# Small products of a hybrid RWKV-7, sparse and dilated attention trunk, laid out anew on the tensor array

## The chip, the cores and the metric

The kernel runs on one core of one Trainium2 chip. The core has a tensor engine (PE, with its weight loads shown as PEld), a vector engine (DVE), a scalar engine (ACT), a general engine (POOL) and a queue engine that issues most DMA transfers (SP). The metric is the device time of one execution in microseconds; a kernel's time is the median of its runs.

## What is computed

Two layers (DEPTH = 2) over 1024 tokens of width 1024, all in float32. Each layer projects the normalised input and feeds the columns to three branches, whose outputs are joined, projected and gated:

```python
for i in range(DEPTH):
    h = rms_norm(x, norm_g[i])
    z = h @ w_in[i]
    z_a, z_b, z_c = split_cols(z, (RWKV_IN_WIDTH, DSA_IN_WIDTH, DIL_IN_WIDTH))
    y_a = rwkv7_branch(z_a, ...)      # 6 heads of 64, a state of 64x64 per head, decay and rate by low-rank "lora"
    y_b = dsa_branch(z_b, ...)        # 4 heads of 64 on one key/value head; the 256 best keys of each query
    y_c = dilated_branch(z_c, ...)    # 3 groups of 2 heads, rates 1, 4, 16, blocks of 128
    x = x + jnp.concatenate([y_a, y_b, y_c], axis=-1) @ w_out[i]
    gate = jax.nn.sigmoid(rms_norm(x, ple_norm_g[i]) @ ple_w_gate[i])
    x = x + gate * (p[i] @ ple_w_proj[i])
return rms_norm(x, final_norm_g)
```

The products that matter here: in `dsa_branch` the scores `q k^T` (the query split in an upper and a lower part of its precision, so 64 features become 128 rows plus 64 more) and the probabilities times `v`; in `dilated_branch` the scores of a block of 128 queries with its own and the previous 128 keys; in `rwkv7_branch` the two lora products `tanh(wd) @ w_up` and `ad @ a_up`, and the scan over time, which is done in chunks of 64 tokens.

## The kernel before

**Stages of a layer.** (1) The tail of the previous layer and the first columns; (2) the projections of all other columns ("z", lines 713 to 737, each product as three of reduced precision), which fill PE until about 505 us in layer 1, beside the index scores and the search for each query's threshold on DVE and ACT (line 579, up to 433 us); (3) the mask of chosen keys on DVE (`dsa_mask`, lines 624 to 645); (4) the attention stage, from about 525 to 773 us: dilated attention (`dil_att`), attention over the chosen keys (`dsa_attend`), the rest of the RWKV chain, then `dil_join`; (5) the tail (line 1695), whose first product (line 334) needs `yT`, the joined outputs, back from memory.

**Who sets the order.** The work is written as streams of generators. `Flow.run` (line 182) plays them against assumed durations, the numbers in `piece(engine, us)`, and takes, among the streams that could start soon, the one of lowest `RANK` (line 38). What it yields is the fixed order of each engine's instructions; on the chip each engine works in this order and waits where an operand is late. `get` and `put` hand out buffers and PSUM banks by tag: "z" and "t" have 2 banks each, "a" has 4. `after` and `done` are events.

**The lines that the change touches.**
- DSA scores: lines 912 and 913, a product on 128 rows and one on 64 rows, for each head and up to 512 keys; 96 pairs in the two layers. Keys are loaded by `load_keys` (line 859).
- DSA values: line 970, probabilities (transposed, `pT`) stay in the array, 64 columns of `v` move; 288 products. Output: lines 976 to 998.
- Dilated scores: `turned` (line 1049) writes each head's queries with zeros in the other head's 64 rows, so that line 1065 uses all 128 rows; 48 units, 22 of them with a previous block (4 products), 26 without (2).
- Lora: line 1263 for the decay (rows 0 to 63), line 1275 for the rate (rows 64 to 127), both through `product` (record at line 1245), for each of 8 token blocks a layer.
- RWKV chain (`rwkv_chain`): for each token block two steps `e` of state read (line 1573), solve (1586) and state update (1596), and its outputs (1618). Lines 1378 (`rwkv_cross`), 1507 (`rwkv_merge`) and 1635 are not changed; they use parts of the array.
- Mask: lines 630 to 643, ten DVE instructions for each of six query blocks a layer.

Of the kernel before, what the change touches and what calls it, by code (L numbers as in the profile page):

```python
# [37 lines left out]
RANK = dict(chain=0, merge=28, inverse=2, cross=3, tokens=3, ahead=3, prep=-2, y=-1, out=6, counts=1.4, search=8,  # L38
            mask=18, products=36, evict=5.5, weights=2.5, embed=25, kept=35, columns=25, index=2, q=36, load=15,
# [64 lines left out]
def after(*event):  # L104
    return "after", event
# [98 lines left out]
def tile_kernel(ctx, tc, x, p, norm_g, w_in, tshift_mu, rwkv_w0, rwkv_w_up, rwkv_a0, rwkv_a_up, rwkv_k_k,  # L204
# [407 lines left out]
    def dsa_mask(mk, d):  # L612
# [11 lines left out]
        for qb in range(2, NT):  # L624
            n, j = (qb + 1) * 128, slice(qb - 2, qb - 1)
            hi, lo = d["hl"][qb]
            yield piece("DVE", 0.2 + n / 1900)
# [3 lines left out]
            DVE.tensor_scalar(tmp, lo, t[:, j], None, OP.is_equal)  # L631
            yield piece("DVE", 0.4 + 2.3 * n / 960)
            DVE.tensor_tensor(bias, bias, tmp, OP.mult)
            DVE.tensor_tensor_scan(tmp, zero.to_broadcast([128, n]), bias, need[:, j], OP.add, OP.subtract)
            yield piece("DVE", 1.45)
            DVE.tensor_scalar(tmp, tmp, 0.0, None, OP.is_ge)
            DVE.tensor_tensor(bias, bias, tmp, OP.mult)
            for src, lim in ((hi, T), (lo, t)):
                yield piece("DVE", 1.1)
                DVE.tensor_scalar(tmp, src, lim[:, j], None, OP.is_gt)  # L640
                DVE.tensor_tensor(bias, bias, tmp, OP.add)
# [9 lines left out]
    def z_streams(i, flow, wp, zp, HT, LT, col, feats, ZT, w1, wtail, d):  # L651
# [61 lines left out]
        def products(it):  # L713
# [5 lines left out]
            for x, c in enumerate(slices):  # L719
                for k in range(8):  # L720
                    if n:
                        yield after("w", 2, (n, k // 2))
                    if kind == "rwkv" or k % 2 == 0:
                        yield piece("PE", 0.7, True)
# [126 lines left out]


    def dsa_attend(flow, opened, d, gate):
# [5 lines left out]
        def load_keys(ka, dl, half):  # L859
# [4 lines left out]
            SP.dma_start(K[half][:64, 1].bitcast(F32), kd[:64, 1, c])  # L864
            SP.dma_start(V[half], vd[:, half * 4:half * 4 + 4])
# [35 lines left out]
        def scores(it):  # L901
# [6 lines left out]
            yield piece("PE", 0.05 + m / 600)  # L908
# [4 lines left out]
            PE.matmul(b, q[:64, h], k[:64, 1, :m], start=False, stop=True)  # L913
# [45 lines left out]
        def values(it):  # L959
            qb, h, c0 = it  # L960
            k0 = c0 // 128
            m = min(4, qb + 1 - k0)
            if h == 0 and k0 == 0:
                yield get("a")
            yield piece("PE", m * 0.214)
            if h == 0 and k0 == 0:
                O[qb] = psa()
            pT = PT.pop(it)
            for k in range(m):
                PE.matmul(O[qb][:, h * 64:(h + 1) * 64], pT[:, k * 128:(k + 1) * 128], V[k0 // 4][:, k],  # L970
                          start=k0 + k == 0, stop=k0 + k == qb)
# [4 lines left out]
        def output(qb):  # L976
            yield after("o", qb)
            yield piece("DVE", 1.03)
            st, sg, o = Q[qb]["st"], Q[qb]["sg"], O.pop(qb)
            DVE.reciprocal(st[:, 3], st[:, 2])  # L980
            y = da.tile([128, 256], F32, name="y")
            DVE.scalar_tensor_tensor(y.rearrange("p (h e) -> p h e", h=4), o[:, :256].rearrange("p (h e) -> p h e", h=4),
                                     0.5, st[:, 3].rearrange("p (h o) -> p h o", o=1).to_broadcast([128, 4, 64]),
                                     OP.mult, OP.mult)
            DVE.tensor_tensor(y, y, sg, OP.mult)
            yield piece("PE", 0.22)
            t = o[:, 256:]
            for j in range(2):
                PE.transpose(t[:, j * 128:(j + 1) * 128], y[:, j * 128:(j + 1) * 128], ident)
            yield piece("ACT", t_act(256))  # L990
            yt = d["dl"].tile([128, 256], F32, name="yt")
            ACT.copy(yt, t)
# [12 lines left out]

    hrow = lambda h: slice(h % 2 * 64, h % 2 * 64 + 64)


    def dil_att(flow, opened):
# [15 lines left out]
        def load(u):  # L1025
            nonlocal dl
            if u == 0:
# [3 lines left out]
                yield piece("POOL", 1.5)  # L1031
                for j in range(3):
                    QK.append(dl.tile([128, 3, 128], F32, name=f"qk{j}"))
                    POOL.memset(QK[j], 0.0)
# [14 lines left out]
        def turned(u):  # L1049
            yield get("qk")  # L1050
            yield piece("ACT", 0.77)
            qk, t = QK[u % 3], T.pop(u)
# [856 lines left out]
```

## Time and profile before

| | us |
|---|---|
| median of 3 runs | 1967.21 (1966.08 to 1974.93) |
| the profiled execution | 1961.57 |
| its span, first to last instruction | 1959.8 |
| PE busy | 1845.0 (94%) |
| DVE busy | 1287.7 (66%) |
| ACT busy | 1062.2 (54%) |
| POOL busy | 633.9 (32%) |
| mean granted clock of the tensor engine | 0.971 |

All profile rows name lines of the kernel ("L970" is line 970). A row of the timeline holds the start of a group of equal instructions, their time from the first start to the last end, the engine, line, operation, output<-inputs, for PE the part of the array used (rows*columns) and the shape, and the count; in brackets the idle time before it and what ended it. Products are pipelined: the time from one row's start to the next row's start is what PE spends on it. A float32 product leaves two records in the timeline, one of reduced precision leaves one.

### The profile page before, as it was taken

To read this page: it belongs to the slowest core of one execution; us is meant where nothing else is said; L and a number is where in the kernel's file an instruction comes from. 1 tells how busy PE (TensorE), PEld (TensorE's weight loads), DVE (VectorE), ACT (ScalarE), POOL (GpSimd) and SP (SyncE) were. 2 spreads that over 40 slices of the span, in tenths; PEclk is the share of its full clock that TensorE was granted. 3 is DMA by queue.
4 is the path that set the end of the run, shared out by engine and by line. 5 is a ranking of instruction groups with operands and counts; after the bars stand their busy time and mean duration, and the time that the engine had idled before them with its cause. 6 is when DMAs were issued, how large, how long until landed. Compare 5 with 4: busy or idle time off the path is not lost. (4 is left out here: it accounts for less than half of the span.)

```text
span 1959.8 us, 40297 instructions
## 1 busy us (share of the span) xinstructions
PE 1845.0 (94%) x15214; PEld 1687.6 (86%) x15214; DVE 1287.7 (66%) x2956; ACT 1062.2 (54%) x2377; POOL 633.9 (32%) x842
## 2 busy tenths in 40 slices
PE   7999999999799997899999999999998999969998
PEld 6888888999798886799998888899997988869998
DVE  4489998898765753215344889997986667432344
ACT  5576666662376864214246766665624868632323
POOL 5422263362232202223224322633613322112322
PEclk9999998999899998899999999999997999979999
DMA  6222323133353324612322223331323523164123
GB/s 195 62 68 88 112 84 101 55 89 98 115 160 96 96 67 137 215 44 66 113 93 60 73 87 105 99 90 52 104 92 111 175 81 108 42 206 130 44 81 114
DMA packets 232410, 196.36 MB, mean 100 GB/s; under 512 B 19284, under 2 KB 204056, under 8 KB 232216
## 3 DMA queue, kind: packets, MB, share of 16 engines
q1 hardware_dynamic: 232216, 193.79, 32.7%
q8 instruction: 120, 1.97, 0.4%
q14 instruction: 74, 0.61, 0.1%
HBM read 128.36 MB, written 65.37 MB: 99 GB/s over the span
## 5 line engine op out<-in xcount | busy, mean ns | idle before, releaser
L334 PE MATMUL z<-wH,HT 128*128 128x256 f32 x1024 | 291.9, 287 | 25.4 <-ACT HT L244 25.4
L735 PE MATMUL z<-wH,HT 128*128 128x256 f32 x1024 | 304.0, 297 | 9.7 <-DVE zt L778 8.2
L336 PE MATMUL z<-wH,LT 128*128 128x256 f32 x1024 | 294.3, 289 | 4.9 <-DVE LT L245 4.9
L335 PE MATMUL z<-wL,HT 128*128 128x256 f32 x1024 | 292.8, 287 | 0.0
L736 PE MATMUL z<-wL,HT 128*128 128x256 f32 x1024 | 291.2, 284 | 0.0
L737 PE MATMUL z<-wH,LT 128*128 128x256 f32 x1024 | 290.9, 284 | 0.0
L701 POOL TENSOR_TENSOR wL<-wraw,wH 128x512 fp32r<-128x512 f32 (+1 forms) x128 | 165.6, 1305 | 266.9 <-ACT wH L689 212.1
L334 PEld LDWEIGHTS z<-wH,HT 128*128 128x128 f32 x1024 | 198.8, 195 | 26.7 <-ACT HT L244 26.5
L735 PEld LDWEIGHTS z<-wH,HT 128*128 128x128 f32 x1024 | 197.3, 193 | 16.3 <-DVE zt L778 9.1
L336 PEld LDWEIGHTS z<-wH,LT 128*128 128x128 f32 x1024 | 198.8, 195 | 7.4 <-DVE LT L245 7.0
L335 PEld LDWEIGHTS z<-wL,HT 128*128 128x128 f32 x1024 | 199.5, 195 | 0.1
L736 PEld LDWEIGHTS z<-wL,HT 128*128 128x128 f32 x1024 | 197.7, 193 | 0.3
L737 PEld LDWEIGHTS z<-wH,LT 128*128 128x128 f32 x1024 | 197.4, 193 | 0.0
L326 POOL TENSOR_TENSOR wL<-wraw,wH 128x512 fp32r<-128x512 f32 (+1 forms) x72 | 100.5, 1414 | 282.4 <-ACT wH L325 267.9
L735 PE MATMUL z<-HT,wH 128*128 128x512 f32 x416 | 165.6, 398 | 0.4 <-DVE zt L757 0.4
L736 PE MATMUL z<-LT,wH 128*128 128x512 f32 x416 | 162.9, 392 | 0.0
L737 PE MATMUL z<-HT,wL 128*128 128x512 f32 x416 | 162.7, 391 | 0.0
L325 ACT CAST wH<-wraw 128x512 fp32r<-128x512 f32 (+1 forms) x72 | 46.8, 650 | 137.6 <-PE z L336 91.8
L579 DVE TENSOR_SCALAR_CACHE_REDUCE junk<-hi,t 128x384 bf16<-128x384 uint16 (+3 forms) x136 | 110.3, 811 | 3.9
L1566 POOL TENSOR_TENSOR sp<-S,PC 64x192 f32<-64x192 f32 x64 | 33.2, 519 | 243.1 <-DVE S L1600 240.7
L579 DVE TENSOR_SCALAR_CACHE_REDUCE junk<-lo,t 128x384 bf16<-128x384 uint16 (+3 forms) x136 | 109.8, 807 | 3.0
L475 DVE SCALAR_TENSOR_TENSOR sc<-rl,iw,sc 128x512 f32<-128x512 f32 (+3 forms) x140 | 106.8, 809 | 2.5 <-ACT rl L462 0.4
(297 smaller groups left out, 4640.0 us busy)
## 6 DMA issues: line engine op xcount, KB each, us to landing
wraw<-in_w_in_dram SPq DMA_DIRECT2D x208, 128.0 KB
zr<-zt SPq DMA_DIRECT2D x52, 256.0 KB
zd<-zt SPq DMA_DIRECT2D x48, 256.0 KB
z<-zd SPq DMA_DIRECT2D x48, 256.0 KB
wraw<-in_w_out_dram SPq DMA_DIRECT2D x32, 256.0 KB
pd<-pe SPq DMA_DIRECT2D x32, 256.0 KB
hn<-yT SPq DMA_DIRECT2D x16, 512.0 KB
wraw<-in_ple_w_gate_dram SPq DMA_DIRECT2D x32, 256.0 KB
```

What stands on the lines that cost most here:

```text
L325: ACT.copy(H[:, :, :n], raw)
L326: POOL.tensor_tensor(L[:, :, :n], raw, H[:, :, :n].bitcast(F32), OP.subtract)
L334: PE.matmul(o, aH, bH, start=j == 0, stop=False)
L335: PE.matmul(o, aH, bL, start=False, stop=False)
L336: PE.matmul(o, aL, bH, start=False, stop=j == n - 1)
L475: DVE.scalar_tensor_tensor(sc[:, c], rl, w, sc[:, c], OP.mult, OP.add)
L579: DVE.tensor_scalar(junk[0][:, :n], hl[qb][lower], col(t, qb), None, OP.is_lt, OP.add, accum_out=col(cnt, qb))
L701: POOL.tensor_tensor(L, RAW.pop(it), H.bitcast(F32), OP.subtract)
L735: PE.matmul(o, aH, bH, start=k == 0, stop=False)
L736: PE.matmul(o, aH, bL, start=False, stop=False)
L737: PE.matmul(o, aL, bH, start=False, stop=k == 7)
L1566: POOL.tensor_tensor(sp[hrow(h)], s0[hrow(h), :, hrow(h)], PC[hrow(h), :, e:e + 1].to_broadcast([64, 3, 64]), OP.mult)
```

## The change

- DSA scores: the second product uses all 128 rows; the upper half of that part of the keys is set to zero once per 512 keys, on POOL.
- DSA values: `v` (64 columns) stays in the array and the transposed probabilities move; two heads go to the upper and lower 64 output rows of one bank. The sum is then already transposed; the gate and the reciprocal are multiplied before the transposes, and the result after them.
- Dilated scores: no zeros; the two heads use rows 0 to 63 and 64 to 127 and write two "a" banks.
- Lora: one block of six products that alternate between the row halves, into two "t" banks.
- State update: six products of 64 output rows instead of three of 128; outputs: one block of twelve products for both halves instead of two of six, at rank 18 instead of -1; the state's part of the output is copied to `Yt` (now 2 buffers) at once.
- Mask: four pairs of DVE instructions become one each; the loads of the attention stages get rank 1.8 instead of 15.
- The assumed durations of these pieces are changed with them.

```diff
-            mask=18, ... y=-1, ... load=15, ...
+            mask=18, ... y=18, ... load=1.8, ...
...
             DVE.tensor_scalar(bias, hi, T[:, j], None, OP.is_equal)
-            DVE.tensor_scalar(tmp, lo, t[:, j], None, OP.is_equal)
-            DVE.tensor_tensor(bias, bias, tmp, OP.mult)
+            DVE.scalar_tensor_tensor(bias, lo, t[:, j], bias, OP.is_equal, OP.mult)
...
-                DVE.tensor_scalar(tmp, src, lim[:, j], None, OP.is_gt)
-                DVE.tensor_tensor(bias, bias, tmp, OP.add)
+                DVE.scalar_tensor_tensor(bias, src, lim[:, j], bias, OP.is_gt, OP.add)
...
+            POOL.memset(K[half][64:, 1].bitcast(F32), 0.0)
...
             PE.matmul(b, q[:, h], k[:, 0, :m], start=True, stop=False)
-            PE.matmul(b, q[:64, h], k[:64, 1, :m], start=False, stop=True)
+            PE.matmul(b, q[:, h], k[:, 1, :m], start=False, stop=True)
...
-                PE.matmul(O[qb][:, h * 64:(h + 1) * 64], pT[:, k * 128:(k + 1) * 128], V[k0 // 4][:, k],
-                          start=k0 + k == 0, stop=k0 + k == qb)
+                for e in range(2):
+                    PE.matmul(O[qb][hrow(e), h // 2 * 128:h // 2 * 128 + 128], V[k0 // 4][:, k],
+                              pT[e][:, k * 128:(k + 1) * 128], start=k0 + k == 0, stop=k0 + k == qb)
...
-            for h in range(2):
-                ACT.copy(qk[hrow(h), h], t[hrow(h), :128])
-            ACT.copy(qk[:, 2], t[:, 128:])
+            ACT.copy(QK[u % 3], T.pop(u).rearrange("p (j t) -> p j t", j=2))
...
-            yield get("a")
+            yield get("a", 2)
...
-                    PE.matmul(B[u][:, h, e * 128:e * 128 + 128], QK[u % 3][:, h], QK[(u - 1 + e) % 3][:, 2],
+                    PE.matmul(B[u][h][:, e * 128:e * 128 + 128], QK[u % 3][hrow(h), 0], QK[(u - 1 + e) % 3][hrow(h), 1],
                               start=True, stop=True)
...
-            yield from product(lambda pr: lora[:64, fc(pr)], lambda pr: wa[:64], "ACT", 0.8, tanh(P, "w0"))
+            for pr in range(3):
+                for e in range(2):
+                    PE.matmul(b[e][:, fc(pr)], lora[hrow(e), fc(pr)], wa[hrow(e)], start=True, stop=True)
...
-                for pr in range(3):
-                    PE.matmul(b[:, fc(pr)], BKt[:, e, fc(pr)], SV[:, e, fc(pr)], start=True, stop=True)
+                for h in range(6):
+                    PE.matmul(up[hrow(h), h // 2], BKt[:, e, hcol(h)], SV[:, e, hcol(h)], start=True, stop=True)
...
-            for e in range(2):
-                yield after("sa", hf, e)
-                for h in range(6):
+            yield after("sa", hf, 1)
+            for h in range(6):
+                for e in range(2):
                     PE.matmul(b[kr(e), hcol(h)], G[:, e, h, kr(e)], SV[:, e, hcol(h)], start=True, stop=True)
```

Since the planner's numbers change, the whole order moves. In the changed kernel's rows the lines are shifted: L974 is the values' product, L1050, L1065, L1101 and L1120 are the dilated turn, scores, transposes and values, L1585, L1600, L1612 and L1629 are the chain's read, solve, update and outputs, L1689 and L1188 are the last transposes of RWKV and of the join.

PE at the end of layer 1's attention stage, before: the last DSA values (L970), the join's and RWKV's transposes, then the tail's first product.

```order
L1187 MATMUL t<-cst,o 128x128 x3
L970 MATMUL a<-v,pT 128x64 x4
L1187 MATMUL t<-cst,o 128x128 x3
L970 MATMUL a<-v,pT 128x64 x4
L1679 MATMUL t<-cst,o_9116 128x128 x3
L1187 MATMUL t<-cst,o 128x128 x3
L970 MATMUL a<-v,pT 128x64 x4
L1187 MATMUL t<-cst,o 128x128 x3
L970 MATMUL a<-v,pT 128x64 x4
L1187 MATMUL t<-cst,o 128x128 x6
L989 MATMUL a<-cst,y 128x128 x2
L334 MATMUL z<-wH,HT 128x256
```

The same place in the changed kernel:

```order
L1600 MATMUL a<-rs,TT 64x64 x6
L1101 MATMUL a<-cst,dpr 128x128 x2
L1612 MATMUL a<-SV,BKt 64x64 x6
L1629 MATMUL a<-SV,G 64x64 x12
L1120 MATMUL a<-z,dpT 128x64 x2
L1050 MATMUL t<-cst,z 128x128 x2
L1065 MATMUL a<-qk_5836 128x128 x2
L1101 MATMUL a<-cst,dpr 128x128 x2
L1120 MATMUL a<-z,dpT 128x64 x2
L1689 MATMUL t<-cst,o_9195 128x128 x3
L1188 MATMUL t<-cst,o 128x128 x24
L334 MATMUL z<-wH,HT 128x256
```

The DSA values no longer stand between the join's transposes; the last dilated unit and the last step of the RWKV chain do stand directly before them.

DVE at the end of the last mask block of layer 1, before: L641 and L640 are of the mask, L643 writes its result; the rest belongs to the RWKV chain (L1578, L1600, L1620), its preparation (L1382) and its output (L1673).

```order
L640 TENSOR_SCALAR junk_635<-lo_624,t 128x1024
L641 TENSOR_TENSOR junk_634<-junk_634,junk_635 128x1024
L1600 TENSOR_TENSOR S_1930<-a,sp 64x3x64 x2
L1382 TENSOR_TENSOR G<-t,cst 128x2x2x128
L1673 TENSOR_TENSOR o_5097<-Yt,ost 128x384
L1578 TENSOR_TENSOR rs<-a,gv 64x384
L1382 TENSOR_TENSOR G<-t,cst 128x2x2x128
L1620 TENSOR_TENSOR Yt<-a,rs 64x384
L643 TENSOR_SCALAR hi_623<-junk_634 128x1024
L1620 TENSOR_TENSOR Yt<-a,rs 64x384
L1600 TENSOR_TENSOR S_1929<-a,sp 64x3x64 x2
```

In the changed kernel L633 to L638 are the mask, L640 writes its result, L1548 and L1556 are of the merge, L775 of the projections, and L1592 and L1615 are the chain:

```order
L633 SCALAR_TENSOR_TENSOR junk_635<-zero,lim,junk_634 128x1024
L635 SCALAR_TENSOR_TENSOR junk_634<-junk_635,junk_634 128x1024
L638 SCALAR_TENSOR_TENSOR junk_634<-hi_623,T,junk_634 128x1024
L1548 TENSOR_TENSOR TT<-t,DT 128x384
L638 SCALAR_TENSOR_TENSOR junk_634<-lo_624,t,junk_634 128x1024
L775 SCALAR_TENSOR_TENSOR zt<-zt,z 128x512
L640 TENSOR_SCALAR hi_623<-junk_634 128x1024
L1556 TENSOR_TENSOR TT<-TT,t 128x384
L1592 TENSOR_TENSOR rs<-a,gv 64x384
L1615 TENSOR_TENSOR S_1951<-a,sp 64x3x64 x2
L775 SCALAR_TENSOR_TENSOR zt<-zt,z 128x512
L1592 TENSOR_TENSOR rs<-a,gv 64x384
```

The first chain step of the second pair of token blocks, with all that follows it, now stands behind the last mask block.

More of the change, by code (lines that the diff above doesn't have):

```diff
@@ L36 @@
 RW, DS, DL = 0, 1664, 2600
-RANK = dict(chain=0, merge=28, inverse=2, cross=3, tokens=3, ahead=3, prep=-2, y=-1, out=6, counts=1.4, search=8,
-            mask=18, products=36, evict=5.5, weights=2.5, embed=25, kept=35, columns=25, index=2, q=36, load=15,
+RANK = dict(chain=0, merge=28, inverse=2, cross=3, tokens=3, ahead=3, prep=-2, y=18, out=6, counts=1.4, search=8,
+            mask=18, products=36, evict=5.5, weights=2.5, embed=25, kept=35, columns=25, index=2, q=36, load=1.8,
             dil=20, join=8, dsa=65)
@@ L626, in dsa_mask @@
             hi, lo = d["hl"][qb]
[L627 removed]
+            yield piece("DVE", 0.2 + n / 770)
             bias, tmp = (a[:, :n] for a in d["junk"])
@@ L1080, in biased @@
             for h in range(2):
-                DVE.tensor_tensor_reduce(pr[:, h, lo:], b[:, h, lo:], mask, -0.125, ROOF, OP.add, OP.min,
+                DVE.tensor_tensor_reduce(pr[:, h, lo:], b[h][:, lo:256], mask, -0.125, ROOF, OP.add, OP.min,
                                          accum_out=o[:, 128 + h:129 + h])
+            yield put("a")
             yield put("a")
@@ L1259, in decay @@
             yield done("w", hf)
-            lora, wa, P, iP = R["lora"], T["wa"], tile_("P"), tile_("iP")
+            lora, wa, P, iP, ta, ke = R["lora"], T["wa"], tile_("P"), tile_("iP"), tile_("ta"), tile_("ke")
             yield piece("ACT", 0.24)
             ACT.activation(wa[:64], wa[:64], AF.Tanh)
-            yield from product(lambda pr: lora[:64, fc(pr)], lambda pr: wa[:64], "ACT", 0.8, tanh(P, "w0"))
+            yield get("t", 2)
+            yield piece("PE", 0.9)
+            b = pst(), pst()
+            for pr in range(3):
+                for e in range(2):
+                    PE.matmul(b[e][:, fc(pr)], lora[hrow(e), fc(pr)], wa[hrow(e)], start=True, stop=True)
+            yield piece("ACT", 0.8)
+            tanh(P, "w0")(b[0])
+            yield put("t")
+            yield piece("ACT", 0.8)
+            tanh(ta, "a0")(b[1])
+            yield put("t")
+            yield done("rate", hf)
             yield piece("DVE", 1.25)
@@ L1272, in icl @@
         def icl():
-            yield after("w", hf)
-            lora, wa, ta, ke = R["lora"], T["wa"], tile_("ta"), tile_("ke")
-            yield from product(lambda pr: lora[64:, fc(pr)], lambda pr: wa[64:], "ACT", 0.8, tanh(ta, "a0"))
+            yield after("rate", hf)
+            ta, ke = T["ta"], T["ke"]
             yield piece("DVE", 1.6)
@@ L1825, in tile_kernel @@
             rk = Pools(None)
-            flow = Flow(t=2, z=2, a=4, raw=3, wHL=2, zt=3, iqS=2, rl=4, sc=2, wk=1, w=1, rv=1, AR=2, BK=2, gv=1, t2=2, G=2, SV=2, BKt=1, XN=1, rs=3,
-                        Yt=1, dz=3, qk=3, dpr=1, dpT=2, pe=3, O=3, qload=2, pr=5, pT=4)
+            flow = Flow(t=2, z=2, a=4, raw=3, wHL=2, zt=3, iqS=2, rl=4, sc=2, wk=1, w=1, rv=1, AR=2, BK=2, gv=1, t2=2, G=2, SV=2, BKt=1, XN=1, rs=2,
+                        Yt=2, dz=3, qk=3, dpr=1, dpT=2, pe=3, O=3, qload=2, pr=5, pT=4)
             flow.free.update(BUSY)
```

92 lines of the change are left out of this document (46 added, 46 removed).

## The prediction

> **What bounds the kernel now.** I read the page first, then the busy time in windows, then the timeline of PE, because a product's rate stands only in the distance between starts: the "mean ns of one" of a pipelined product is its delay.
>
> ```profile
> span 1959.8 us, 40297 instructions
> PE 1845.0 (94%) x15214; PEld 1687.6 (86%) x15214; DVE 1287.7 (66%) x2956; ACT 1062.2 (54%) x2377; POOL 633.9 (32%) x842
> ```
>
> ```profile
> 150.00:200.00 50.00, 50.00 (x221) 41.20 (x220) 45.13 (x92) 33.59 (x58) 13.69 (x23) 1.00 0.28 84
> 200.00:250.00 50.00, 48.13 (x283) 42.03 (x282) 47.25 (x120) 33.97 (x67) 14.67 (x19) 1.00 0.37 107
> 600.00:650.00 50.00, 48.44 (x493) 42.30 (x489) 32.29 (x98) 34.38 (x105) 11.94 (x17) 1.00 0.33 91
> 750.00:800.00 50.00, 31.81 (x204) 30.30 (x202) 14.38 (x28) 16.33 (x29) 12.82 (x11) 0.73 0.63 195
> 850.00:900.00 50.00, 50.00 (x422) 50.00 (x421) 17.77 (x22) 18.06 (x33) 18.30 (x25) 1.00 0.15 49
> ```
>
> The columns are span, PE, PEld, DVE, ACT, POOL, granted clock. PE is full nearly everywhere. From 600 us to 650, the attention stage, it has 48.44 of 50 us and no other engine over 35: a microsecond of PE taken out there is one of the span, until something else is late. Around 200 us DVE (47.25) is as full, from the search. At the layer's end (750 to 800) PE waits and its clock falls to 0.73. Full windows give rates: 221 products of 512 columns in 50 us are 0.226 us each, 422 of 256 columns 0.118.
>
> **The change part by part: prices.**
>
> ```profile
> 586.12 0.92 PE L1507 MATMUL t<-DT,XN 64*64 64x64 f32 x24
> 586.86 0.87 PE L1507 MATMUL t<-XN,rs 64*64 64x64 f32 x24
> 635.65 0.91 PE L1618 MATMUL a<-SV,G 128*64 128x64 f32 x12
> 636.50 0.55 PE L1401 MATMUL t<-cst,zv 128*128 128x128 f32 x3
> 637.10 0.83 PE L1596 MATMUL a<-SV,BKt 128*128 128x128 f32 x6
> 637.86 0.91 PE L1618 MATMUL a<-SV,G 128*64 128x64 f32 x12
> 646.08 0.93 PE L1245 MATMUL t<-wa,lora 64*128 64x128 f32 x6
> 646.94 0.33 PE L1416 MATMUL t<-cst,BK 128*128 128x128 f32 x1
> ...
> 661.42 1.16 PE L1378 MATMUL t<-AR,BK 64*128 64x128 f32 x16
> 662.51 0.44 PE L1100 MATMUL a<-cst,dpr 128*128 128x128 f32 x2
> 663.06 0.51 PE L912 MATMUL z<-kq,q 128*128 128x512 f32 x1
> 663.50 0.50 PE L913 MATMUL z<-kq,q 64*128 64x512 f32 x1
> 663.93 0.66 PE L1119 MATMUL a<-z,dpT 128*128 128x64 f32 x4
> 664.42 1.06 PE L970 MATMUL a<-v,pT 128*128 128x64 f32 x8
> 665.31 0.39 PE L1047 MATMUL t<-cst,z 128*128 128x128 f32 x2
> 666.21 0.31 PE L912 MATMUL z<-kq,q 128*128 128x128 f32 x1
> 666.45 0.32 PE L913 MATMUL z<-kq,q 64*128 64x128 f32 x1
> 666.70 0.43 PE L970 MATMUL a<-v,pT 128*128 128x64 f32 x2
> ```
>
> "64*128" is the part of the array used, rows by columns. A float32 product leaves two records. Whole array: L970's eight take 0.89 us, 0.111 a record. Two products on different rows share the time: L1378's 16 records on alternating halves take 1.09, not 16 x 0.111 = 1.78. Of the 1.09, 16 x 0.056 = 0.90 is the products; 0.19 is extra. The four records of L1119 after L913 take 0.49, not 0.44, so a neighbour pays too. I price an isolated block of another array form at 0.3 us (0.19 plus 0.1 around it, an estimate). The Trainium skill, "TensorEngine Tiling (Array Packing)", Key Properties, says that changing the tiling mode drains the engine; by that it speaks for the scores and against the values, the state update and the dilated scores, and the trace agrees. Were the change of form free, the scores would gain nothing and the values, lora, outputs, state update and dilated scores, at the overlapped rate alone, 32 + 11 + 11 + 10 + 16 = 80 us.
>
> - **DSA scores on full rows.** A pair of 512 columns takes 0.44 + 0.43 us, two plain products 2 x 0.226 = 0.45: 0.42 saved, x48. At 128 columns 0.24 + 0.25 against 2 x 0.111: 0.27, x16. The 32 pairs of 256 and 384 columns lie between, 0.35. Sum 20.2 + 4.3 + 11.2 = 36 us. The two clears of half a key tile run on POOL, idle two thirds of the time, and precede a load: zero.
>
> ```profile
> L970 PE MATMUL a<-v,pT 128*128 128x64 f32 x576 | 82.3, 284 | 1.4 <-ACT pT L956 1.4
> ```
>
> - **Values transposed.** 288 products (576 records) of 0.223 are 64 us. Now 64 columns of V stay and 128 columns of pT move; two heads use the two column halves. No row shows such a pair. From below: both halves together take one whole-array product's time, 144 x 0.223 = 32. From above: no overlap, 64. I take the overlap, since L1507, whose tiles differ in rows and columns, runs 24 records in 0.74 us where L1618 on one half needs 0.85 for 12. With 48 blocks at 0.3 (14 us) the gain is 32 - 14 = 18 us; the other end is a loss of 14.
> - **Outputs.** Two blocks of 0.85 us become one of 24 records, which by L1507 takes 0.80 with its changes: 0.9 and a neighbour's 0.1 saved, x16 = 16 us. Without overlap 2.
> - **Lora.** Two blocks of 0.86 + 0.1 become one of 12 records, by L1378 1.09 - 4 x 0.056 = 0.87, + 0.1: 0.95 x 16 = 15 us. The second tanh now stands earlier on ACT, behind nothing that is late.
> - **State update.** 0.76 us for six records becomes 12 of half width: 0.19 + 6 x 0.062 (L1507's 0.74/12) + 0.1 = 0.66: 0.1 x 32 = 3 us. Without overlap 1.04, a loss of 9.
> - **Dilated scores.** Eight records 0.89 become 0.29 + 0.45 (22 blocks); four, 0.44, become 0.29 + 0.22 (26): +3 - 2 = 1 us. ACT saves two copies a unit; no wait there is long enough to count.
> - **Ranks, slots, Yt.** L1618's counterpart still stands right behind the chain's step in the order: zero. The loads' rank moves only SP issues: zero.
>
> The sum on PE is 36 + 18 + 16 + 15 + 3 + 1 = 89 us. Blocks that stand beside each other share a change: I take 90.
>
> **Mask on DVE.**
>
> ```profile
> 432.77 0.16 DVE L588 TENSOR_TENSOR lim<-cnt,lim 128x6 f32<-128x6 f32 x1
> 522.62 0.41 DVE L643 TENSOR_SCALAR hi<-junk 128x1024 bf16<-128x1024 bf16 x1
> ```
>
> ```profile
> L604 DVE SCALAR_TENSOR_TENSOR lo<-hi,T,lo 128x1024 uint16<-128x1024 uint16 x2 | 2.6, 1284 | 0.1
> L641 DVE TENSOR_TENSOR junk<-junk,junk 128x1024 bf16<-128x1024 bf16 x4 | 2.8, 692 | 0.1
> L1578 DVE TENSOR_TENSOR rs<-a,gv 64x384 f32<-64x384 f32 x32 | 17.8, 555 | 24.6 <-ACT rs L1576 24.2
> ```
>
> Four pairs of instructions become four joined ones. By L604 a joined one costs 1.28 us at 1024; a pair costs L641's 0.69 and a compare, bounded by L643's 0.41 and by another 0.69. So -0.1 to +0.2 each, 48 of them: -5 to +9 us on DVE, taken as zero. More matters where the mask stands: from the search's end (432.77) to the last mask (522.62) pass 90 us, and in the new order the chain's steps, a preparation and an output that stood between (four L1578 at 0.56, and some twenty more of like size) come behind it: 24 x 0.56 = 13 us of work, and the waits for PE before it. I put the mask's end 13 to 20 us earlier. The dilated stage, gated by it, starts earlier beside the last projections. That is what lets the saving of the first half of a layer, where DVE is full, count at all.
>
> **Given back at the layer's end.**
>
> ```profile
> 740.78 0.29 DVE L1127 TENSOR_TENSOR O<-a,z 128x128 f32<-128x128 f32 x1 [0.32 <-PE a L1119]
> ...
> 750.50 0.17 DVE L1156 TENSOR_TENSOR w<-o 128x16 f32<-128x16 f32 x1 [2.84 <-DMA o<-od]
> 752.32 0.18 DVE L1157 TENSOR_TENSOR w<-w,o 128x16 f32<-128x16 f32 x1 [1.65 <-DMA o<-od]
> ```
>
> ```profile
> 753.54 0.66 PE L947 MATMUL a<-cst,pr 128*128 128x128 f32 x4 [2.96 <-ACT pT L956]
> ...
> 782.06 0.58 PE L334 MATMUL z<-wH,HT 128*128 128x256 f32 x1 [9.22 <-ACT HT L244]
> ```
>
> Now the last dilated unit ends at 741, its sums travel to memory and back until 752.3, and DSA products fill PE meanwhile; PE loses 2.96 us at 753 and 9.22 before the tail. In the new order DSA's values end before the last two dilated units and the last chain step; after the last unit PE has only 27 transposes (3 us). Its 11.5 us of travel, about 4 of weights and first transposes, and the 9 before the tail then stand bare: 24 - 3 = 21 us idle, now some 15 with the slowed clock. The two last units, with nothing between their steps, add about 6. So 12 us a layer, 0 to 20, are lost: 2 x 12 = 24 us off the 90. I take 22, since the mask's earlier end helps the start of the stage.
>
> The forecast is 90 - 22 = 68 us. The profiled execution took 1961.57 us, its span 1959.8; the median of the runs is 1967.2, 5.6 higher, and I expect the same distance after. 1967.2 - 68 = 1899 us.
>
> **The rivals.**
>
> 1. *The end exposes nothing more* (the sums' travel falls on the chain's last steps): the whole 90 us, 1877. Against it stands the order itself. 12%.
> 2. *Column halves overlap in part or not at all.* Values lose up to 32 us, outputs 14, state 12: gain 68 - 58 = 10 at worst, about 20 since the longer PE work covers the end; half of it gives 39. So 1913 to 1947. For it: no row shows two tiles that differ in columns alone. Against: L1507. 12%. The Trainium skill, "TensorE: Matmul & The Clock Gate", Part 3, lists 2.38 times for three column tiles; an estimate of 1.6 for two would cut the gain by about 14 us, to 1913.
> 3. *The RWKV chain binds instead of PE.*
>
> ```profile
> PE a L1586 <- DVE rs L1578: 10.6, 15, 2.5
> ```
>
> ```profile
> 607.97 0.78 PE L1573 MATMUL a<-S,AR 128*128 128x128 f32 x5
> 718.93 0.78 PE L1573 MATMUL a<-S,AR 128*128 128x128 f32 x5
> ```
>
>    Between the two starts, of the third and fourth pair of token blocks, lie 111 us. In the new order about 85 us of PE work stands between them. If preparation, inverse and merge take 100 us whatever PE does, 15 us a layer are lost: a gain of 36, 1931. For it: that chain runs through DVE, ACT and POOL in small steps. Against: the longest of PE's waits for it is 2.5 us, so PE, not the chain, was late. 13%.
> 4. *Slower: banks.* The dilated scores now take two of the four "a" banks at once, which DSA's transposes and outputs and the chain use too. PE works in order, so a block without its second bank holds all that follows.
>
> ```profile
> PE a L947 <- ACT pT L956: 6.1, 2, 3.1
> ```
>
>    That is the longest wait on an "a" bank's readers now, 3 us. At 3 us in each of the 48 blocks the kernel would lose 146 against 68 gained: 2045. It decides from 1.4 us a block. Against: banks are given out by the same planner. 3%.
> 5. *No change*: rivals 2 and 3 together, gain under 10 us: 3%.
>
> **How the numbers follow.** The forecast's own case (gain 51 to 84 us, 1883 to 1916) has 57%. The range leaves out rival 4, no change, and the far ends of 1 and 2: 1875 to 1936. About 0.5%, 10 us, is what a measurement here tells from no change. Faster: 57 + 12 + 12 + 13 = 94%; same 3%; slower 3%.
>
> **What would show it.** Right: score pairs near 0.45 us; eight records of values near 0.45 to 0.5 us plus the change; 24 output records in 0.8; the tail's first product near 748 us instead of 782, after an idle of PE over 15 us; the last mask before 512 us. Wrong: values records at 0.11 each (rival 2); PE under 46 of 50 us in the attention windows with chain steps waited for (rival 3); waits before the dilated scores (rival 4).

## The result and the profile after

The changed kernel takes 1920.3 us in the median (1919.5 to 1924.5), the kernel before 1968.8 in the runs beside it: a ratio of 0.9754, 95% interval 0.9726 to 0.9782, or 48 us saved. The forecast was 68. Beside the later runs the kernel before came out at 1968.2 to 1969.3, so medians from different rounds are set against each other below. The profiled executions lie closer together (1961.6 and 1924.5, 37 us), because the one before was below its median and the one after was the highest of its runs.

The page of the changed kernel, the span and the busy times:

```profile
span 1922.7 us, 40427 instructions
PE 1764.9 (92%) x15406; PEld 1606.5 (84%) x15406; DVE 1278.8 (67%) x2892; ACT 1038.0 (54%) x2281; POOL 639.2 (33%) x840
```

PE is busy for 80 us less, but the span is only 37 shorter: 43 us of new idle time. To see where, I cut layer 1 at the first state read of each pair of token blocks (L1573 before, L1585 after) and at the tail's first product. Busy time in these stretches, before (columns: stretch, its length, PE, PEld, DVE, ACT, POOL, granted clock, DMA share, GB/s):

```profile
0.00:370.20 370.20, 346.70 (x2275) 306.88 (x2276) 287.07 (x609) 234.59 (x464) 152.00 (x227) 0.99 0.33 99
370.20:495.20 125.00, 121.89 (x1254) 116.43 (x1253) 109.31 (x248) 58.64 (x129) 46.26 (x60) 1.00 0.27 82
495.20:608.00 112.80, 101.64 (x1014) 91.59 (x1012) 75.70 (x205) 72.26 (x200) 36.63 (x42) 0.92 0.45 136
608.00:718.90 110.90, 109.12 (x1077) 92.90 (x1076) 74.53 (x251) 81.53 (x237) 21.91 (x29) 1.00 0.32 91
718.90:782.00 63.10, 48.78 (x397) 42.83 (x396) 26.28 (x71) 28.79 (x68) 14.58 (x18) 0.87 0.37 105
```

and after:

```profile
0.00:362.80 362.80, 334.18 (x2179) 295.73 (x2180) 277.57 (x595) 226.90 (x452) 141.46 (x215) 0.98 0.33 97
362.80:495.60 132.80, 126.61 (x1338) 121.17 (x1337) 124.08 (x248) 64.55 (x140) 60.18 (x72) 0.99 0.29 87
495.60:601.50 105.90, 100.92 (x1150) 90.23 (x1149) 69.67 (x203) 73.39 (x199) 36.07 (x40) 0.97 0.54 162
601.50:700.00 98.50, 89.01 (x1048) 72.43 (x1048) 72.32 (x234) 70.50 (x188) 22.26 (x29) 0.98 0.29 80
700.00:763.70 63.70, 37.97 (x398) 30.78 (x396) 24.08 (x72) 30.36 (x73) 17.80 (x20) 0.77 0.45 128
```

The second stretch became longer (125 to 133 us; DVE is busy for 124.08 of them), the third and fourth shorter by 7 and 12, and the last kept its length although PE has 11 us less to do there: it waits 26 of 64 us. The stretches are cut at events and hold different work before and after (see the counts), so a longer stretch alone doesn't say that PE lost time in it.

Three numbers for each kernel make this exact. From all records of PE: its busy time, each record counted until the next one starts; of that, half of what lies in stretches where the granted clock is 0.5 is called **half clock**, the rest **work**; what lies between records is **idle**. Their sum is 18 to 19 us under the span (the head and the end). The positions are of layer 1, in us: p1 to p4 are the state reads named above, then the first and the last values product of the dilated units, and the tail's first product.

| kernel | median | ratio to before (95%) | work | idle | half clock | p1 | p2 | p3 | p4 | dilated | tail |
|---|---|---|---|---|---|---|---|---|---|---|---|
| before | 1968.8 | 1 | 1805.0 | 96.0 | 40.0 | 370 | 495 | 608 | 719 | 544-740 | 782 |
| changed | 1920.3 | 0.9754 (0.9726-0.9782) | 1723.4 | 139.9 | 41.5 | 363 | 496 | 602 | 700 | 512-735 | 764 |
| *parts alone* | | | | | | | | | | | |
| e1_scores | 1948.9 | 0.9911 (0.9881-0.9941) | 1782.8 | 111.3 | 31.8 | 367 | 492 | 601 | 711 | 540-740 | 775 |
| e2_values | 1965.8 | 0.9988 (0.9970-1.0007) | 1784.5 | 114.9 | 44.2 | 367 | 492 | 607 | 726 | 543-742 | 784 |
| e3_rwkv | 1977.7 | 1.0044 (1.0015-1.0072) | 1770.3 | 127.4 | 51.7 | 369 | 510 | 626 | 737 | 535-741 | 787 |
| e4_dil | 2021.7 | 1.0260 (1.0189-1.0332) | 1806.8 | 119.7 | 64.6 | 368 | 493 | 605 | 712 | 547-788 | 811 |
| e5_mask | 1976.6 | 1.0056 (1.0035-1.0076) | 1807.5 | 96.5 | 51.6 | 367 | 497 | 615 | 734 | 528-740 | 789 |
| *one part left out* | | | | | | | | | | | |
| e10_no_dil | 1943.9 | 0.9873 (0.9799-0.9948) | 1729.0 | 147.9 | 38.5 | 363 | 496 | 613 | 724 | 519-718 | 768 |
| e7_no_rwkv | 1943.2 | 0.9888 (0.9841-0.9934) | 1764.0 | 129.7 | 28.7 | 367 | 497 | 615 | 715 | 513-744 | 780 |
| e8_no_mask | 1963.0 | 0.9971 (0.9948-0.9994) | 1722.4 | 158.8 | 65.7 | 369 | 510 | 623 | 731 | 531-764 | 789 |
| e11_no_lora | 1918.9 | 0.9746 (0.9711-0.9781) | 1739.5 | 119.5 | 43.0 | 366 | 487 | 599 | 705 | 516-741 | 766 |
| *order and clock* | | | | | | | | | | | |
| e6_oldranks | 1948.3 | 0.9897 (0.9832-0.9962) | 1728.4 | 148.0 | 53.6 | 362 | 499 | 610 | 715 | 512-752 | 780 |
| t1_dil_first | 1973.2 | 1.0022 (0.9988-1.0056) | 1724.2 | 169.8 | 59.1 | 362 | 495 | 628 | 743 | 510-737 | 789 |
| f1_warm | 1919.0 | 0.9750 (0.9721-0.9779) | 1753.3 | 109.1 | 37.5 | 362 | 495 | 601 | 699 | 511-734 | 766 |

The profiles are one execution each. f1_warm keeps the changed kernel's order and adds products at the layers' ends, and its stretch from the tail to layer 2's first state read came out with 7 us less idle and half clock than the changed kernel's. Part of that may be the added products' effect, so such sums can carry up to some 7 us. Its work holds 30 us of the added products.

The changed blocks in the timeline of PE after; read the distance from each start to the next:

```profile
595.40 0.88 PE L974 MATMUL a<-pT,v 128*64 128x128 f32 x12
596.21 0.49 PE L1065 MATMUL a<-qk 64*128 64x128 f32 x4
...
605.42 0.57 PE L1612 MATMUL a<-SV,BKt 128*64 128x64 f32 x12
605.92 0.44 PE L1050 MATMUL t<-cst,z 128*128 128x128 f32 x2
606.20 0.60 PE L947 MATMUL a<-cst,pr 128*128 128x128 f32 x4
606.55 0.48 PE L912 MATMUL z<-kq,q 128*128 128x512 f32 x1
606.87 0.40 PE L913 MATMUL z<-kq,q 128*128 128x512 f32 x1
607.11 0.83 PE L1585 MATMUL a<-S,AR 128*128 128x128 f32 x6
...
611.43 0.87 PE L1629 MATMUL a<-SV,G 128*64 128x64 f32 x24
612.23 0.66 PE L1120 MATMUL a<-z,dpT 128*128 128x64 f32 x4
...
615.17 1.09 PE L974 MATMUL a<-pT,v 128*64 128x128 f32 x16
616.20 0.66 PE L947 MATMUL a<-cst,pr 128*128 128x128 f32 x4
...
639.27 0.94 PE L1269 MATMUL t<-wa,lora 64*128 64x128 f32 x12
640.14 0.66 PE L947 MATMUL a<-cst,pr 128*128 128x128 f32 x4
```

State update 0.50 us (forecast 0.66), outputs 0.80 (0.80), lora 0.87 (0.87), a score pair 0.32 + 0.24 (0.45 forecast), sixteen records of values 1.03: sixteen whole-array records would take 1.78 at the prediction's 0.111, so the column halves overlap.

The mask on DVE, the search's end and the last mask's end, after:

```profile
425.97 0.16 DVE L588 TENSOR_TENSOR lim<-cnt,lim 128x6 f32<-128x6 f32 x1
494.10 0.42 DVE L640 TENSOR_SCALAR hi<-junk 128x1024 bf16<-128x1024 bf16 x1
```

Now 68 us pass between them, not 90. The end of layer 1 on PE, after (last dilated unit, last RWKV transposes, first join transposes, tail; in brackets PE's wait and its cause):

```profile
734.17 1.01 PE L1120 MATMUL a<-z,dpT 128*128 128x64 f32 x4 [0.46 <-ACT dpT L1109]
738.64 0.87 PE L1689 MATMUL t<-cst,o 128*128 128x128 f32 x3 [3.46 <-DVE o L1683]
747.56 0.87 PE L1188 MATMUL t<-cst,o 128*128 128x128 f32 x3 [8.05 <-DVE o L1175]
...
763.69 0.58 PE L334 MATMUL z<-wH,HT 128*128 128x256 f32 x1 [5.05 <-ACT HT L244]
```

And the longest groups of waits after (total, times, longest):

```profile
PE z L732 <- DVE zt L775: 23.2, 4, 8.7
...
PE t L1390 <- DVE BK L1335: 11.0, 4, 4.2
```

The first (8.2 us before, at L735) lies in the projections. Its longest in layer 1, before and after:

```profile
318.77 0.58 PE L735 MATMUL z<-wH,HT 128*128 128x256 f32 x1 [3.60 <-DVE zt L778]
```

```profile
322.67 0.55 PE L732 MATMUL z<-wH,HT 128*128 128x256 f32 x1 [8.74 <-DVE zt L775]
```

After, PE waits for an eviction that stands on DVE behind 13 us of RWKV's small steps (from L1459 at 309 us to L775 at 322).

### The profile page after: what moved, and what is told of

The parts are those of the page before. It is cut to its first block, busy times and chain, and to the rows that moved or that the text cites. A ratio compares the mean times of both kernels' runs of the same rounds, so it can differ in the third digit from the quotient of the medians.

```text
span 1922.7 us, 40427 instructions
## 1 busy us (share of the span) xinstructions
PE 1764.9 (92%) x15406; PEld 1606.5 (84%) x15406; DVE 1278.8 (67%) x2892; ACT 1038.0 (54%) x2281; POOL 639.2 (33%) x840
## 5 line engine op out<-in xcount | busy, mean ns | idle before, releaser
L732 PE MATMUL z<-wH,HT 128*128 128x256 f32 x1024 | 309.5, 302 | 23.2 <-DVE zt L775 23.2
L698 POOL TENSOR_TENSOR wL<-wraw,wH 128x512 fp32r<-128x512 f32 (+1 forms) x128 | 172.3, 1354 | 280.7 <-ACT wH L686 197.7
L732 PEld LDWEIGHTS z<-wH,HT 128*128 128x128 f32 x1024 | 201.0, 196 | 30.4 <-issue 18.3
L326 POOL TENSOR_TENSOR wL<-wraw,wH 128x512 fp32r<-128x512 f32 (+1 forms) x72 | 100.3, 1413 | 270.8 <-ACT wH L325 267.7
L732 PE MATMUL z<-HT,wH 128*128 128x512 f32 x416 | 165.4, 398 | 0.0
```

The source lines that it names most:

```text
L326: POOL.tensor_tensor(L[:, :, :n], raw, H[:, :, :n].bitcast(F32), OP.subtract)
L698: POOL.tensor_tensor(L, RAW.pop(it), H.bitcast(F32), OP.subtract)
L732: PE.matmul(o, aH, bH, start=k == 0, stop=False)
```

## The experiments

**Theory 1**, the prediction's: each part is worth what it takes off PE, less what the layer's end exposes. **Theory 3**, the rival: the streams wait on each other's steps, and a part's gain comes back as waits. The first runs put each part by itself into the kernel before.

**DSA scores alone.**

```diff
+            POOL.memset(K[half][64:, 1].bitcast(F32), 0.0)
-            yield piece("PE", 0.05 + m / 600)
+            yield piece("PE", 0.05 + m / 1150)
-            PE.matmul(b, q[:64, h], k[:64, 1, :m], start=False, stop=True)
+            PE.matmul(b, q[:, h], k[:, 1, :m], start=False, stop=True)
```

> The kernel before with one part of the change: the DSA scores on full rows (with the cleared half tiles and the new assumed duration). The timeline of the changed kernel shows L912 and L913 together at 59.2 us against 69.8 - 0.0 before for 96 pairs, 49.9 with the neighbours' share, so the part takes 20 us off PE and not the 36 of the prediction. Theory 1 (in the attention stage PE is the bound, and each part is worth what it takes off PE): 20 us faster, within 5. Theory 2 (the prediction's own price holds and the rest was lost elsewhere): 30 to 36 us faster. Theory 3 (the attention stage is as much held by the steps that wait on each other as by PE, so that a part's gain comes back as waits): under 10 us faster, with PE's idle time up by 10 or more.

(The 59.2 and the "- 0.0" in it are slips: 49.9 against 69.8 are meant.) Measured 1948.9 us: 17.5 less than before (0.9911). Work is 22 less, idle 15 more and half clock 8 less. A pair in its timeline:

```profile
615.61 0.48 PE L913 MATMUL z<-kq,q 128*128 128x512 f32 x1
615.93 0.39 PE L914 MATMUL z<-kq,q 128*128 128x512 f32 x1
616.16 0.60 PE L1101 MATMUL a<-cst,dpr 128*128 128x128 f32 x4
```

The second product takes 0.23 us, the first 0.32 (median of 37 pairs), not the 0.226 of a full window; the pair before took 0.41 + 0.42 in the median of 42, not 0.87. So a pair saves 0.28, not 0.42. The time fits theory 1 with this price, and not the prediction's price; but idle rose by more than 10, as theory 3 has it, and about half of that came back as less half clock. So one run of this part doesn't prove theory 1.

**DSA values and their output alone** (the hunk on L970 in the diff of the change, and the output's, which multiplies the gate and the reciprocal ahead of the transposes and the result behind them).

> The kernel before with one part of the change: DSA values transposed with two heads side by side, and the output that follows. In the changed kernel this part takes 31 us less of PE (70.2 to 38.7 us by starts). Theory 1 (each part is worth what it takes off PE): 31 us faster, less what the layer's end exposes when the DSA values end sooner, 0 to 12 us a layer: 10 to 31, with PE's idle time at the end of the layers up by the difference. Theory 2 (prediction: the change of array form costs 0.3 us a block): 18 us faster. Theory 3 (waits come in its place all over the attention stage): under 10 us faster.

Measured 1965.8 us, 2 less than before, which is within the noise (0.9988, 0.9970 to 1.0007). The work falls by 20.5 us (forecast 18), and 23 come back in the profile: idle 19 more, half clock 4 more, nearly all of it net between p3 and p4 of the two layers. The work is near the prediction's price and the time isn't: theory 3.

**RWKV parts alone.**

```diff
-            ... y=-1, ...
+            ... y=18, ...
-            yield from product(lambda pr: lora[:64, fc(pr)], lambda pr: wa[:64], "ACT", 0.8, tanh(P, "w0"))
+                    PE.matmul(b[e][:, fc(pr)], lora[hrow(e), fc(pr)], wa[hrow(e)], start=True, stop=True)
...
+                    PE.matmul(up[hrow(h), h // 2], BKt[:, e, hcol(h)], SV[:, e, hcol(h)], start=True, stop=True)
...
+                    PE.matmul(b[kr(e), hcol(h)], G[:, e, h, kr(e)], SV[:, e, hcol(h)], start=True, stop=True)
```

> The kernel before with the RWKV parts of the change: lora in one block, state update in halves, outputs in one block at rank 18, Yt in two buffers. In the changed kernel these take 38 us less of PE (lora 14.5, outputs 13.1, state 9.9). Theory 1 (each part is worth what it takes off PE): 30 to 38 us faster. Theory 3 (the RWKV stream is held by its own steps on DVE, ACT and POOL, and its first half stands beside a full DVE): 0 to 15 us faster, and PE's waits for DVE and ACT in the projections and the attention stage up by 20 or more, as in the whole change (L732 waiting for the eviction L775, L1390 for L1335).

Measured 1977.7 us, 9 slower (1.0044), with 35 us less work (34 forecast). Idle rises by 31, half clock by 12. More than half of this (24 us in the two layers) stands between p1 and p2. In layer 1 this stretch grows from 125 to 141 us; its columns, and its longest wait:

```profile
369.00:510.00 141.00, 129.60 (x1344) 123.88 (x1343) 120.45 (x268) 61.97 (x138) 51.45 (x66) 0.95 0.27 82
```

```profile
PE z L735 <- DVE zt L778: 8.2, 1, 8.2
```

PE is idle for 11 of it, where it was for 3, and 8.2 are one wait for an eviction on DVE, as in the whole change. That is theory 3, at a place where DVE is busy for 120 of 141 us.

**Mask alone**, with the loads' rank and the assumed durations of the mask and the projections.

```diff
-            ... load=15, ...
+            ... load=1.8, ...
+            DVE.scalar_tensor_tensor(bias, lo, t[:, j], bias, OP.is_equal, OP.mult)
...
+                DVE.scalar_tensor_tensor(bias, src, lim[:, j], bias, OP.is_gt, OP.add)
```

> The kernel before with the joined mask instructions, the loads' rank 1.8 and the assumed durations of the mask and the projections alone; PE's work is that of before. Prediction and theory 1: the mask's end comes 13 to 20 us earlier, DVE's busy time stays within 10 us, and the time within 10 us of before (the 9 us that PE waits at 500 to 550 us of layer 1 may go). Theory 3 (the order of the new assumed durations itself costs: PE waits for evictions at 300 us as in the whole change): 5 to 20 us slower.

Measured 1976.6 us, 11 slower (1.0056); DVE's busy time is the same (1285 us). The mask ends 23 us earlier (500), the dilated units start 16 us earlier (528), p3 and p4 come 7 and 15 later, idle stays, half clock rises by 12. So the earlier mask helps nothing by itself. The time is within theory 3's 5 to 20 us, and at the edge of theory 1's 10.

**Dilated part alone.**

```diff
-            yield get("a")
+            yield get("a", 2)
-            B[u] = psa().rearrange("p (h c) -> p h c", h=2)
+            B[u] = psa(), psa()
...
+                    PE.matmul(B[u][h][:, e * 128:e * 128 + 128], QK[u % 3][hrow(h), 0], QK[(u - 1 + e) % 3][hrow(h), 1],
```

> The kernel before with the dilated part of the change alone: scores without zeros, two heads on the row halves, two banks taken at once. Its PE work falls by 4 to 7 us (L1065 33.4 to 26.4 us by starts in the whole change). In its order the last dilated unit is the last work on PE before the join, as in the whole change; in the kernel before DSA values stood behind it. Theory A (two banks at once hold the dilated units back in the planner's order, so that the last unit, its sums' travel and the join stand bare at the layer's end): PE's idle time up by 10 us a layer, 10 to 20 us slower. Theory B (the end is set by the RWKV chain and not by the dilated units): within 5 us of before or up to 7 faster.

The clearing on POOL and two of the three copies a unit on ACT fall away as well, and the assumed durations are the shorter ones.

Measured 2021.7 us, 51 slower (1.026), far past both: idle 24 more, half clock 25 more, work 2 more. Its chain is on time (p4 712, before 719), but the dilated units end at 788 us instead of 740, alone and bare:

```profile
782.21 1.12 PE L1115 MATMUL a<-z,dpT 128*128 128x64 f32 x4 [0.46 <-ACT dpT L1104]
...
787.25 1.12 PE L1115 MATMUL a<-z,dpT 128*128 128x64 f32 x4 [0.46 <-ACT dpT L1104]
800.28 0.90 PE L1183 MATMUL t<-cst,o 128*128 128x128 f32 x3 [11.92 <-DVE o L1170]
```

The last two stand 5 us apart, and nothing else is left for PE. What changed for them is that their scores ask for two of the four banks: the planner serves that only when two lie free at once, and whoever asks for one takes his before (so its code says; it was not tested apart). That is rival 4's scarcity in the order instead of on the chip.

Alone, by their ratios, scores, values, RWKV, dilated part and mask are worth -17.5, -2, +9, +51 and +11 us, a loss of 51; together they gain 48. So the question became how they hang together, and parts were left out of the whole.

**Without the dilated part** (the diff above taken back).

> The changed kernel with the dilated part as before: one bank, zeros in the other head's rows, all 128 rows. In its order the last dilated unit stands some 15 us of PE work ahead of the end again, with DSA values and the chain's last step behind it. Theory A (two banks at once hold the dilated units back, and that exposes the end): PE's idle time at the layers' end falls by 8 to 10 us a layer, against 4 to 7 us more work: 1900 to 1912 us. Theory B (the chain's last step, which still stands at the end, sets it): 1918 to 1930 us.

Measured 1943.9 us, 24 slower than the changed kernel. The dilated units do end 17 us sooner (718), but the chain's p4 comes 24 later (724): theory A falls, and the time lies above theory B's range too. The idle from p4 to the tail stays, 23.7 us against 25.7. Whichever stream is last, what follows it is bare.

**The two old ranks.**

```diff
-            ... y=18, ... load=1.8, ...
+            ... y=-1, ... load=15, ...
```

> The changed kernel with the two ranks of before (y -1, load 15). The prediction priced the ranks at nothing. If that holds: within 10 us of 1920. If the outputs' rank is what holds back the chain (its first to second pair takes 133 us from start to start in the changed kernel, 125 before) the period of the first pair falls to 125 and the time by 10 to 16 us; if it is what lets the chain pass in the attention stage, the time rises by 10 or more.

Measured 1948.3 us: the two ranks, priced at nothing, are worth 28 us here. Work is 5 us more, idle 8, half clock 12; the dilated units end 17 us later. Which of the two ranks counts was not set apart.

**Dilated units ahead of the chain.**

```diff
-            dil=20, ...
+            dil=-3, ...
```

> The changed kernel with the dilated units' rank lowered from 20 to -3, so that they go ahead of the RWKV chain where both could start. In its order the last dilated unit and the last DSA values stand some 15 us of PE work ahead of the end, and the chain's last step is last. Theory A (the end was exposed by the dilated units): 8 to 10 us a layer less idle at the end, 1900 to 1910 us. Theory B (the chain sets the end; pushed back by the dilated units it ends later still): 1920 to 1935 us.

Measured 1973.2 us, 53 more than the changed kernel. The dilated units end at 737 as ever, and the chain is 43 us later at p4. Theory B, and more than it expected.

**Without the mask part** (the part of e5_mask taken back, the loads' rank with it).

> The changed kernel with the mask's instructions, the assumed durations of mask and projections, and the loads' rank as before. By itself that part cost 11 us (on the kernel before). Theory C (the parts hang together: two banks at once slow the dilated units down, and it is the mask's earlier end that starts them 30 us sooner, at 512 instead of 544 us, so that they still end with the chain): without it the dilated units start near 545 us and end 20 to 40 us after the chain's last step, bare; 1945 to 1980 us. Theory D (parts add up): 1910 us.

Measured 1963.0 us: the part that cost 11 us alone is worth 43 in the whole. The dilated units start at 531, and end after the chain's last solve (L1603):

```profile
749.13 0.91 PE L1603 MATMUL a<-rs,TT 64*64 64x64 f32 x12 [0.60 <-DVE rs L1595]
763.62 1.12 PE L1123 MATMUL a<-z,dpT 128*128 128x64 f32 x4 [0.46 <-ACT dpT L1112]
```

Theory C holds in its main point; the lag is 15 us, less than the 20 to 40 expected. But it is not all: p2 comes at 510 as in e3_rwkv, and at 496 with both parts, so the mask part also makes up for what the RWKV parts cost before p2. The loads' rank is not what does either: with it put back alone beside the other rank (e6_oldranks) the dilated units start at 512 and p2 comes at 499. How much of the 43 us it holds besides was not set apart.

**Without the RWKV parts.**

> The changed kernel without its RWKV parts (lora, state update, outputs and their rank as before). By itself that part cost 9 us, with 35 us less PE work at full clock and 31 us more idle. In the whole: if its PE work counts (the chain is passed by nothing else), 35 us more work and some 10 to 20 less idle: 1935 to 1950 us. If it gives back everything here too: 1905 to 1920 us, with the first to second chain pair at 125 us from start to start instead of 133.

Measured 1943.2 us: 41 us more work, 10 less idle, 13 less half clock. Here the parts are worth 23 us, as the first of the two cases expected.

**Without the lora part.**

```diff
+            yield from product(lambda pr: lora[:64, fc(pr)], lambda pr: wa[:64], "ACT", 0.8, tanh(P, "w0"))
-                    PE.matmul(b[e][:, fc(pr)], lora[hrow(e), fc(pr)], wa[hrow(e)], start=True, stop=True)
```

> The changed kernel with the two lora products as before, each in its own block. PE's work rises by 14.5 us. Theory E (the joined lora, with the second tanh ahead of the decay's work, is what delays PE in the projections, where DVE is full: 9 us a layer more idle before the second chain pair): the idle there falls back by 6 to 9 us a layer and the time stays within 6 us of 1920. If lora is not the cause: idle as in the changed kernel and 10 to 15 us slower than 1920.

Measured 1918.9 us, the same as the changed kernel, with 16 us more work and 20 less idle. The first two stretches of layer 1 again:

```profile
0.00:366.00 366.00, 344.56 (x2253) 305.18 (x2254) 278.35 (x606) 231.88 (x461) 147.21 (x221) 0.98 0.32 98
366.00:487.00 121.00, 116.26 (x1233) 110.16 (x1232) 109.57 (x231) 59.31 (x130) 52.53 (x66) 0.99 0.30 89
```

PE rests 21.4 + 4.7 us in them; in the changed kernel 28.6 + 6.2. The wait of 8.74 us for the eviction is nearly gone:

```profile
317.22 0.58 PE L732 MATMUL z<-wH,HT 128*128 128x256 f32 x1 [1.03 <-DVE zt L775]
```

Theory E holds in that joining lora is worth nothing in the whole and brings this wait. Whether the second tanh is the step that does it was not set apart.

**Filling PE's rests at the layer's end.** The last rests lie in half clock. Is it the clock that costs?

```diff
+        def warm(n, *event):
...
+            for _ in range(n):
+                PE.matmul(b, Q[NT - 1]["q"][:, 0], K[1][:, 0], start=True, stop=True)
...
+        flow.add(-9, warm(28, "ends", NT - 1))
+        flow.add(-9, warm(16, "joined", 5))
+        flow.add(-9, warm(22, "joined", NT - 1))
```

> The changed kernel, every instruction in the same order, with 66 products of 512 columns put into three idle stretches of PE at each layer's end (28 after the chain's last transposes, 16 and 22 around the last of the join's transposes); they write a bank that nobody reads, and leave nothing out. The granted clock is 0.5 there for some 35 of 55 us in the changed kernel. Theory F (the half clock after idle costs what the full work in it loses: 5 to 6 us at each layer's end and as much behind it): the clock is full at the tail's start, and the time 4 to 12 us less than 1920. Against: the clock does not follow these products, or PE's end isn't what is late there: within 3 us of 1920, or slower by the products that don't fit the gaps, up to 6.

Measured 1919.0 us (0.9750): no gain.

```profile
738.30 9.23 PE L1020 MATMUL z<-kq,q 128*128 128x512 f32 x28
...
766.33 0.39 PE L334 MATMUL z<-wH,HT 128*128 128x256 f32 x1 [1.13 <-ACT HT L244]
```

The half clock at the end of layer 1 shrinks from 34 us (734 to 751, 755 to 772) to 18 (733 to 744, 757 to 761, 768 to 771), and the tail starts no earlier: at 766.3, against 763.7. It waits for its operand `HT`, which ACT writes. In the changed kernel ACT waited for a transfer there, in f1_warm until the last of the added products had ended (5.28 us, and 4.58 in layer 2). The changed kernel, then f1_warm:

```profile
762.59 1.05 ACT L244 CAST HT<-hn 128x1024 fp32r<-128x1024 f32 x1 [1.74 <-DMA hn<-yT]
```

```profile
765.24 1.04 ACT L244 CAST HT<-hn 128x1024 fp32r<-128x1024 f32 x1 [5.28 <-PE z L1020]
```

So the added products themselves held the tail up by some 3 us. Filling the rests in this way gains nothing, but the run doesn't say what the half clock costs: what a faster clock won may be hidden by this delay. Theory F stays open. No version that was tried beats the changed kernel; this one and the one without the lora part equal it.

## Why the prediction was nearly right

The time lies in the range, but above the 1883 to 1916 us of the forecast's own case, so the number alone doesn't show that the mechanism was right.

**The sum of work: right in size, 82 us for 90.** One term was far off. The scores gave 22 us, not 36: 0.28 us a pair, since the new pair's first product behind float32 work takes 0.32, and the old pair took 0.83 and not 0.87. The values gave 20.5 for 18: the twelve-record blocks (0.81 us) and the sixteen-record ones (1.03) show 0.056 a record and 0.14 for the change of form inside the block. The values' own work fell by 27.6 us in e2_values, so products beside them took 7 more, 0.15 a block: together near the 0.3 forecast. With the columns overlapping in full, rival 2 is out. The Trainium skill, "TensorE: Matmul & The Clock Gate", Part 3, gives 2.38 for three column tiles; this trace shows 2.0 for two once the 0.14 is set apart. RWKV's 34 became 35, with errors in it that offset: the state update's own work fell by 8 us in e3_rwkv, not 3, the outputs' by 14, not 16, lora's by 14, not 15. The dilated part's 1 lies between -2 (alone) and +6 (in the whole).

**The layer's end: right.** The step forecast 24 us off in two layers. From p4 to the tail idle rose by 11.4 and 9.2 and half clock by 0 and 3.4: 24. The bare stretch after the last unit came as described, with idle of 3.5, 8.1, 4.8 and 5.1. But the reason given, that the dilated units end last, is only half of it: with them ended 17 us sooner (e10_no_dil) the chain's end lay just as bare.

**The step that failed** is the one from "I take 90" to the forecast: it takes off only the layer's end, and so let every microsecond of PE count. In the first half of the layers, to p2, work fell by 23 us over both, and idle and half clock rose by 29 (9.1 and 8.8 idle, 2 and 8.6 half clock): in layer 1 p2 stands where it stood, at 496 and 495 us. The mask's earlier end was to make that saving count; lora's 15 us were worth nothing (e11_no_lora), and the wait for the eviction (L732) makes up most of the new idle time. From p3 to p4 another 18 came back in many small waits. PE is busy for 89 of 98.5 us there, about 45 of 50, which is the sign that the prediction gave for rival 3 (under 46). But the waits belong to several streams; the two longest sums in layer 1:

```profile
PE a L947 <- ACT pT L956: 2.0, 2, 1.0
PE t L1390 <- DVE BK L1335: 1.5, 1, 1.5
```

The first is of the DSA attention, the second of RWKV's preparation. RWKV's preparation and chain hold 3.3 of the 9 us. So rival 3, which foresaw 30 us over two layers, is at most a part of it, and no run set it apart. Against these 47 stand 24 us won from p2 to p3, where PE's rests at 505 to 535 us and their half clock went. The longest of them before:

```profile
513.86 1.54 PE L1586 MATMUL a<-rs,TT 64*64 64x64 f32 x12 [2.52 <-DVE rs L1578]
```

The mask's end came at 494.5 us (forecast before 512), and the prediction had put only 2 us on it. So: 82 of work, 24 lost at the end, 29 in the first half, 18 from p3 to p4, 24 won back behind p2: 35, against 37 of the profiles. That the total came within 20 us of the forecast is in part luck: a loss of 47 us that it didn't have stood against a gain of 24, of which it had 2.

**The zero for ranks, slots and `Yt`** failed too. The two ranks alone move 28 us, more than the dilated part or RWKV's (24 and 23); slots and `Yt` were not tested apart. The tail's first product came at 764, not 748, with all of this.

**Rival 4**, on the chip, didn't come: no wait before the dilated scores is over 1.5 us. By the planner's code its place was the order (e4_dil). Two small slips in the prediction's sums change nothing here: 68 less two times 15 is 38, not 36, and 48 blocks of 3 us are 144, not 146.

What stays open: why the parts are worth so different amounts alone and together, beyond the dilated part and the mask, and what the half clock costs. Scores and values were not left out of the whole. Each part also changes the planner's order, and no run took work off PE and kept the order.

## What to carry over

A microsecond off the fullest engine counts only where nothing else is nearly as full, and an engine at 94% may have stages where it is not the bound; price a part by the stage that it stands in, and ask which stream ends the stage. Where a planner sets the order, a part measured alone tells little about the whole: here the parts alone sum to a loss of 51 us and the whole gains 48. Leaving one part out of the whole doesn't add up either: the dilated part, RWKV's and the mask part are worth 24, 23 and 43 us there, 90 together. It does show which parts need each other.

## What the hardware showed unexpectedly

**The clock stayed at half while PE was busy.** In e5_mask, after this wait:

```profile
684.56 0.69 PE L1097 MATMUL a<-cst,dpr 128*128 128x128 f32 x2 [1.65 <-ACT pT L953]
```

the busy time of 684.5 to 704 us, with the clock behind POOL's:

```profile
684.50:704.00 19.50, 18.94 (x88) 18.36 (x89) 9.54 (x43) 7.95 (x27) 0.09 (x1) 0.50 0.17 50
```

PE is busy for 18.94 of 19.5 us and the granted clock is 0.50. All that PE does there is float32 products of 64 and 128 columns; before and after stand products of reduced precision as well, at full clock. The products are slow in fact: eight records of L967 take 1.60 us there (from 685.04 to 686.64) and 0.84 behind it (from 704.79 to 705.63). Yet the clock was full again from 704.2 us on, while the next product of reduced precision came only here:

```profile
708.36 0.50 PE L909 MATMUL z<-kq,q 128*128 128x512 f32 x1
```

So their absence alone doesn't explain it. The Trainium skill, "TensorE: Matmul & The Clock Gate", Part 1, says that a window of about 3.4 us of sustained work releases the clock; by PE's busy time this trace does not agree. What is counted as work was not tested.

**A product of 512 columns and reduced precision takes 0.32 us behind float32 products**, and 0.23 behind one of its own kind (e1_scores).
